# Linear attention's decay levels in three visits of TensorE a layer instead of four, and a rule for who waits for several PSUM banks

## The chip, the cores and the metric

The kernel runs on one core of a Trainium2 chip. The metric is device time in microseconds of one execution, the median of the runs. Five engines work side by side, each through a queue of its own: TensorE (PE in the profile, with its weight loads PEld), VectorE (DVE), ScalarE (ACT), GpSimd (POOL) and SyncE (SP), which here issues nearly all DMAs.

## The reference

Two layers over 256 positions of width 2048, all in float32. Each layer projects its input once and splits the result into three groups: chunked softmax attention (A, 8 heads), gated linear attention (B, 4 heads with keys of 64 and values of 128) and attention to 256 memory tokens (M, 4 heads). The outputs are gated, concatenated, projected, added to the residual and normalized. What matters here is the part of B inside a chunk of 64 positions:

```python
b = jnp.cumsum(gc, axis=1)
decay = jnp.exp(-jnp.abs(b[:, :, None] - b[:, None, :]))
attn = jnp.einsum('bihd,bjhd,bijhd->bhij', qc, kc, decay)
o_intra = jnp.einsum('bhij,bjhv->bihv', attn, vc)
```

The decay depends on i, j and the feature d, so the scores are not one product of matrices. The kernel splits the 64 x 64 pairs by levels. At a level of size s, the pairs (i, j) lie on the two sides of the middle of a block of 2s positions; with respect to that middle the decay is a product of a factor of i and a factor of j, so the level's scores are one product of decayed keys and decayed queries. Sizes 32, 16, 8, 4, 2 and 1 cover all pairs but the diagonal, which has no decay. That makes seven kinds: -1 (the diagonal) and levels 0 to 5. Each kind's product is computed for all pairs, and a mask picks those that belong to it.

## The kernel before, in words

**The stream of weights.** Nearly all time goes to products with weights. Each weight piece is loaded by DMA (`raw`), rounded by ACT to a high part `wh` (line 261) and completed by DVE with a low part `wl` (line 268). TensorE then multiplies the parts with the input's parts. `take()` hands out the next piece and keeps the high parts three and the low parts two pieces ahead. These operations carry a high priority, so that on ACT and DVE they go ahead of other work that is ready.

**Order.** The order of instructions on TensorE and on SP is the program's own. On ACT and DVE it is fixed when the program is built, by priority and by a forecast of when the operands are ready; on the chip each engine works through its queue in that order.

**Ticks.** After each weight piece the loop calls `tick()`. The smaller work is written as generators: each `next()` issues some instructions, and the number that it yields says after how many ticks it wants to go on. `tick()` first steps those `aside` (the generator `gla` of linear attention, and some helpers), then those `active`: at most two heads at a time, taken in order from `waiting`. `finish(gens)` ticks until the named generators are done; the first use of it in a layer's later part is in the gate of group B.

**Counting.** Call the moment of `beside(gens[0] + others)` tick 0. Ticks 1 to 8 belong to `values(2)`, 9 to 16 to `values(3)` (pieces of 388 columns), 17 to 24 to the projection of further heads, 25 to 32 to the memory queries, 33 on to the gates. Attention head pairs step at these ticks: scores (A) 9, 17, 25, 33; softmax one tick later; transposes of the weights (line 737) four ticks after A; values six ticks after A.

**`gla`.** Lines 533 to 709. It transposes the low-rank gate input, multiplies by the gate matrix, forms the running sums `b_` and, with `distance(lev)` (a subtraction on DVE, line 576, then abs and exp on ACT, lines 578 and 579) and `decayed(dd)` (two products on DVE, lines 584 and 585), the decayed keys and queries of a level. Then it visits TensorE four times, `VISITS`: kinds (-1, 0), (1, 2), (3, 4) and (5). In the first visit four transposes of the keys (line 606) go ahead, and ACT copies them out (line 607). A visit takes two banks `pb` (three in the last), issues 32 matmuls of 64 x 64 x 64 per kind into them, kind i in the columns from 256 i, and has DVE read the result: kind -1 by line 636, the others by a predicated copy, line 638, two of them per kind. The last visit also issues the state's products. After a visit the next visit's levels are prepared, a tick for each step. A tick after the last visit, the combining step takes four banks; a last step five ticks later transposes the result.

**Banks.** PSUM has eight banks; the smaller work shares banks 4 to 7, through the list `free`: `banks(n)` takes the first n, `release` appends them at the end. A bank that is taken again must have been read by whoever was to read it; the build adds the waits. The list is a matter of the program's order, not of time: it is run through while the program is written out. `scratch` gives one of eight rotating SBUF tiles.

In this kernel every caller of `banks` issues its matmuls and the reads of them and releases the banks within the same step, for instance

```python
pb, = yield from banks(1)
mm(ps[:, pb, 0:128], q[:, 0:128], k[:, 0:128], True, True)
mm(ps[:, pb, 128:384], q[:, 128:256], k, True, True)
s = scratch([P, 384])
dve.scalar_tensor_tensor(s, ps[:, pb, :384], SCALE, bias[h], op0=ALU.mult, op1=ALU.add)
release(pb)
```

Of the kernel before, what the change touches and what calls it, by code (L numbers as in the profile page):

```python
# [16 lines left out]
P = 128  # L17
# [3 lines left out]
CH = 64  # L21
# [3 lines left out]
RMS_EPS = 1e-6  # L25
SCALE = P ** -0.5
LEVELS = (32, 16, 8, 4, 2, 1)
VISITS = ((-1, 0), (1, 2), (3, 4), (5,))
PART_B = "WB" * 12
PART_A = "TW" * 16  # L30
QUARTERS = (3, 2)
# [21 lines left out]
def hybrid_trunk_kernel(  # L53
# [23 lines left out]
    ps = psp.tile([P, 8, 512], F32, name="ps")  # L77
# [3 lines left out]
    def nm(s):  # L81
        uid[0] += 1
        return f"{s}_{uid[0]}"

    def mm(o, l, r, start, stop):
        pe.matmul(o, l, r, start=start, stop=stop, skip_group_check=True)  # L86

    def scratch(shape, dtype=F32):
        return sc.tile(shape, dtype, name=nm("sc"), tag="sc")
# [33 lines left out]

    free = [4, 5, 6, 7]

    def banks(n):
        while len(free) < n:
            yield 1
        return [free.pop(0) for _ in range(n)]

    def release(*bs):
        free.extend(bs)
# [397 lines left out]
        later(pool.dma_start(ng, norm_g[l]))  # L530
        return gb, ng

    def gla(gb, ng, gq, gk, asv, yraw):
# [38 lines left out]
        def distance(lev):  # L572
            s = LEVELS[lev]
            bm = b_.rearrange("p (g c) -> p g c", c=2 * s)
            dd = scratch([P, 512])
            dve.tensor_tensor(dd.rearrange("p (g c) -> p g c", c=2 * s), bm,
                              bm[:, :, s - 1:s].to_broadcast([P, 512 // (2 * s), 2 * s]), op=ALU.subtract)
# [4 lines left out]
        def decayed(dd):  # L582
            kl = scratch([P, 512])
            dve.tensor_tensor(kl, gkf, dd, op=ALU.mult)
            dve.tensor_tensor(dd, gqf, dd, op=ALU.mult)
            return kl, dd

        dd = distance(0)
# [4 lines left out]
        dve.tensor_tensor(qe, gqf, eb, op=ALU.mult)  # L593
        yield 1
        ready = [(gkf, gqf), decayed(dd)]
        yield 3

        kdT = yraw[:, 0:2].rearrange("p h (g c) -> p (h g) c", c=P)
        st = hd.tile([P, 3, 2, P], F32, name=nm("st"), tag="st")
        for v, levels in enumerate(VISITS):  # L600
            last = v == len(VISITS) - 1
            if v == 0:
                pt, = yield from banks(1)
                for t in range(2):
                    for b in range(2):
                        pe.transpose(ps[:, pt, (t * 2 + b) * P:(t * 2 + b + 1) * P], kd[:, b * T + t * P:b * T + t * P + P], ident)  # L606
                act.copy(kdT, ps[:, pt].rearrange("p (g c) -> p g c", c=P))
# [12 lines left out]
            if last:  # L620
                kv = (pb[2], pb[1])
                for c in (0, 1, 2):
                    rs = slice((c % 2) * 64, (c % 2) * 64 + 64)
                    t = c // 2
                    for b in range(2):
                        for par in range(2):
                            h = 2 * b + par
                            mm(ps[par * 64:par * 64 + 64, kv[c % 2], (t * 2 + b) * P:(t * 2 + b + 1) * P],
                               kdT[rs, t * 2 + b, par * 64:par * 64 + 64],
                               asv[rs, t, 16 + h * P:16 + (h + 1) * P], True, True)  # L630
            for i, lev in enumerate(levels):
                o = 256 if last else i * 256
                for par in range(2):
                    pv = ps[:, pb[par], o:o + 256].rearrange("p (g c) -> p g c", c=CH)
                    if lev < 0:
                        dve.tensor_tensor(pairs[par], pv, eye.unsqueeze(1).to_broadcast([P, 4, CH]), op=ALU.mult)
                    else:
                        dve.copy_predicated(pairs[par], lmask[:, lev].unsqueeze(1).to_broadcast([P, 4, CH]), pv)
            if last:
                for c in range(3):  # L640
                    src = ps[:, kv[c % 2]].rearrange("p (g c) -> p g c", c=P)[:, (c // 2) * 2:(c // 2) * 2 + 2]
                    if c == 0:
                        dve.tensor_copy(st[:, 0], src)
                    else:
                        for b in range(2):
                            dve.scalar_tensor_tensor(st[:, c, b], st[:, c - 1, b], elast[:, b * 4 + c:b * 4 + c + 1],
                                                     src[:, b], op0=ALU.mult, op1=ALU.add)
            release(*pb)
            if not last:
                ready = []  # L650
# [15 lines left out]
        for g in range(4):  # L666
            t, b = g // 2, g % 2
# [5 lines left out]
        for odd, even in ((1, 2), (3, None)):  # L673
            for b in range(2):
                for c in (odd, even):
                    if c is not None:
                        for par in range(2):
                            rs = slice(par * 64, par * 64 + 64)
                            g = (c // 2) * 2 + b
                            mm(ps[place(par, c % 2), by[par], g * P:(g + 1) * P],  # L680
                               qe[rs, b * T + c * CH:b * T + (c + 1) * CH], st[rs, c - 1, b], True, True)
        for half in range(2):
            for par in range(2):
# [3 lines left out]
                o = on[par][hs, g0:]  # L687
# [12 lines left out]
        for par in range(2):  # L700
# [5 lines left out]
            o = ps[:, pt].rearrange("p (b t h c) -> p h b t c", b=2, t=2, h=2)  # L706
# [266 lines left out]
    gens = []  # L973
    for l in range(L):
        last = l == L - 1
# [32 lines left out]
        gq = hd.tile([P, 2, T], F32, name=nm("gq"), tag="gq")  # L1008
        gk = hd.tile([P, 2, T], F32, name=nm("gk"), tag="gk")
# [4 lines left out]
        gp = gla_inputs(l)  # L1014
        asv = per.tile([P, 2, 1552], F32, name=nm("asv"), tag="asv")
# [40 lines left out]
        yraw = [per.tile([P, 4, T], F32, name=nm("yr"), tag=f"yr{i}") for i in range(4)]  # L1056
# [212 lines left out]
```

## Time and profile before

| what | value |
|---|---|
| median of 3 runs | 912.76 us (912.55 to 913.89) |
| profiled execution, own time | 913.39 us |
| its span | 911.4 us |
| instructions | 14553 |
| mean granted TensorE clock | 0.999 |
| matmuls of linear attention's levels, 64 x 64 | 448 in two layers |

The span runs from the first to the last instruction of the profiled execution. "Busy" is the time in which an engine had an instruction under way; on TensorE successive matmuls overlap, so that the distance between two starts is a better measure of a cost than a duration. A row of the timeline gives the start, the duration from the first start to the last end of the merged instructions, engine, line, operation, output and operands, shape and count; in brackets stands the idle time ahead of it and what ended it. In the code a float32 matmul is one call; on TensorE it shows as two instructions. A row of the waits reads "who waits <- for whom: total us, times, longest".

### The profile page before, as it was taken

The page shows a single profiled execution, that of the slowest core. Times are in us where ns is not written, and L with a number is a line of the kernel's source. Part 1 is how long each engine was busy: PE and PEld are TensorE (multiplying, and loading weights), DVE is VectorE, ACT ScalarE, POOL GpSimd, SP SyncE. Part 2 cuts the span into 40 slices and gives each one's busy share as a digit, 9 for nine tenths or more (in the row PEclk, how much of TensorE's full clock was granted, in tenths as well). Part 3 has the DMA queues.
Part 4 walks back from the last instruction along what each step waited for, and adds up shares of the span by engine and source line. Part 5 has one row for each costly group of instructions (what it writes and reads, how often), then busy time and mean ns, then how long its engine had stood idle before and what let it go on. Part 6 is the DMA issues. An engine that isn't in the chain of part 4 may idle for free.

```text
span 911.4 us, 14553 instructions
## 1 busy us (share of the span) xinstructions
PE 903.2 (99%) x5491; PEld 795.3 (87%) x5491; DVE 717.9 (79%) x995; ACT 551.8 (61%) x809; POOL 13.6 (1%) x32
## 2 busy tenths in 40 slices
PE   9999999999999999999999999999999999999997
PEld 7889989998888888888888899999988888888885
DVE  5697688698766777799979767886886778778996
ACT  5675655576576675555559655556756667566540
POOL 1000000000000000000000000000000000100000
PEclk9999999999999999999999999999999999999999
DMA  8868786775445446876775787666754565776652
GB/s 298 293 195 288 262 266 206 236 253 180 160 145 161 159 161 187 289 272 223 236 243 167 206 291 254 223 196 186 218 177 134 178 192 185 273 277 232 229 190 93
DMA packets 64294, 196.21 MB, mean 215 GB/s; under 512 B 7008, under 2 KB 9568, under 8 KB 64224
## 3 DMA queue, kind: packets, MB, share of 16 engines
q1 hardware_dynamic: 63200, 193.08, 64.9%
q0 software_dynamic: 1024, 2.21, 0.8%
q8 instruction: 43, 0.70, 0.3%
q14 instruction: 27, 0.22, 0.1%
HBM read 193.16 MB, written 2.10 MB: 214 GB/s over the span
## 4 chain that ended last, share of the span: by engine, by line
PE 98%; DVE 1%; DMA 0%; ACT 0%; issue 0%; SPq 0%; DVEq 0%
PE ps L86 96%; PE ps L737 1%; DVE wl L268 0%; DMA raw<-w 0%; PE ps L833 0%; PE ps L775 0%; PE ps L704 0%; DVE sz L498 0%; DVE x L268 0%; ACT wh L261 0%; PE ps L606 0%; ACT res L877 0%; PE ps L541 0%; DVE term L260 0%; ACT wh L360 0%
## 5 line engine op out<-in xcount | busy, mean ns | idle before, releaser
L268 DVE TENSOR_TENSOR wl<-raw,wh 128x1024 fp32r<-128x1024 f32 (+1 forms) x313 | 364.8, 1169 | 118.5 <-PE ps L86 71.1
L261 ACT CAST wh<-raw 128x1024 fp32r<-128x1024 f32 (+1 forms) x313 | 313.9, 1008 | 233.4 <-PE ps L86 125.3
L86 PE MATMUL ps<-x,wh 128*128 128x512 f32 x1408 | 445.0, 397 | 0.0
L86 PEld LDWEIGHTS ps<-x,wl 128*128 128x128 f32 x1408 | 264.2, 188 | 63.2 <-DVE wl L268 1.0
L86 PE MATMUL ps<-x,wl 128*128 128x256 f32 x1408 | 277.5, 279 | 0.3 <-DVE wl L268 0.3
L86 PE MATMUL ps<-wh,x 128*128 128x512 f32 (+2 forms) x856 | 246.5, 369 | 0.9 <-ACT wh L360 0.9
L86 PEld LDWEIGHTS ps<-x,wh 128*128 128x128 f32 x1408 | 219.2, 189 | 1.6 <-issue 0.3
L86 PEld LDWEIGHTS ps<-wh,x 128*128 128x128 f32 x856 | 155.5, 188 | 19.7 <-ACT wh L360 1.1
L86 PE MATMUL ps<-wl,x 128*128 128x512 f32 (+2 forms) x428 | 157.8, 369 | 0.1
L86 PEld LDWEIGHTS ps<-wl,x 128*128 128x128 f32 x428 | 80.3, 188 | 10.5 <-DVE wl L268 0.6
L261 ACT CAST wh<-term 128x776 fp32r<-128x776 f32 (+1 forms) x39 | 36.0, 924 | 51.2 <-DVE term L260 43.3
L268 DVE TENSOR_TENSOR wl<-term,wh 128x776 fp32r<-128x776 f32 (+1 forms) x39 | 41.5, 1065 | 12.7 <-PE ps L86 12.0
L260 DVE TENSOR_TENSOR term<-term,term 128x776 f32<-128x776 f32 (+1 forms) x39 | 41.3, 1060 | 0.2 <-DMA term<-w 0.2
L86 PE MATMUL ps<-wh,s 128*128 128x512 f32 (+1 forms) x144 | 41.2, 367 | 0.0
L86 PEld LDWEIGHTS ps<-wh,s 128*128 128x128 f32 x144 | 25.8, 188 | 3.1
L86 PE MATMUL ps<-wl,s 128*128 128x512 f32 (+1 forms) x72 | 26.6, 370 | 0.3 <-DVE wl L268 0.3
L498 DVE SCALAR_TENSOR_TENSOR sz<-ps,sz 128x512 f32<-128x512 f32 x24 | 16.4, 687 | 5.0 <-ACT sz L497 4.1
L728 ACT ACTIVATE sc<-sc,mx 128x128 f32<-128x128 f32 (+1 forms) x32 | 14.2, 444 | 8.2 <-DVE mx L726 8.2
L86 PE MATMUL ps<-wh,sc 128*128 128x388 f32 x64 | 16.5, 338 | 0.0
L86 PEld LDWEIGHTS ps<-wl,s 128*128 128x128 f32 x72 | 13.5, 188 | 2.3 <-DVE wl L268 0.8
L1119 DVE TENSOR_TENSOR yr<-sz,yr 128x512 f32<-128x512 f32 x16 | 11.0, 687 | 4.6 <-ACT sz L1117 4.6
L1117 ACT ACTIVATE sz<-sz 128x512 f32<-128x512 f32 x16 | 10.1, 632 | 7.1 <-DVE sz L498 7.0
(222 smaller groups left out, 713.9 us busy)
## 6 DMA issues: line engine op xcount, KB each, us to landing
raw<-w SPq DMA_DIRECT2D x254, 512.0 KB, 4.3
raw<-w SPq DMA_DIRECT2D x64, 388.0 KB, 3.8
term<-w SPq DMA_DIRECT2D x24, 388.0 KB, 4.3
term<-w SPq DMA_DIRECT2D x15, 512.0 KB, 5.3
bias<-relw SPq DMA_DIRECT2D x16, 192.0 KB, 3.9
res<-xT SPq DMA_DIRECT2D x4, 512.0 KB, 6.9
res<-xn SPq DMA_DIRECT2D x4, 512.0 KB, 5.4
raw<-memT SPq DMA_DIRECT2D x4, 512.0 KB, 4.5
```

The source lines that it names most:

```text
L86: pe.matmul(o, l, r, start=start, stop=stop, skip_group_check=True)
L260: in_order(dve.tensor_tensor(d.raw, d.raw, d.plus, op=ALU.add))
L261: act.copy(d.hi, d.raw)
L268: in_order(dve.tensor_tensor(d.lo, d.raw, d.hi.bitcast(F32), op=ALU.subtract))
L498: dve.scalar_tensor_tensor(dst, a, scale, dst, op0=ALU.mult, op1=ALU.add)
L728: act.activation(s[:, own[t]], s[:, own[t]], AF.Exp, bias=mx[:, t:t + 1], accum_out=zs[:, t:t + 1])
L737: pe.transpose(ps[:, pt, i * P:(i + 1) * P], s[:, i * P:(i + 1) * P], ident)
L1117: act.activation(sz, sz, AF.Silu)
L1119: dve.tensor_tensor(yraw[i][:, j:j + 2], sz, yraw[i][:, j:j + 2], op=ALU.mult)
```

## The change

`VISITS` has three entries: (-1, 0, 1), (2, 3, 4) and (5). Visits 0 and 1 take four banks; the third kind goes to the second two of them. Level 1 is now prepared ahead of visit 0, two ticks before it, and one tick is added to the wait. Two of the tiles for the third level of visit 1 are halves of `yraw[3]` (the memory heads' output, written later) instead of scratch tiles. `banks` notes who asks for more than one bank in `wanted`, and whoever asks for one bank waits as long as somebody is noted there.

```diff
-VISITS = ((-1, 0), (1, 2), (3, 4), (5,))
+VISITS = ((-1, 0, 1), (2, 3, 4), (5,))
...
+    wanted = []
+
     def banks(n):
-        while len(free) < n:
+
+        if n > 1:
+            wanted.append(n)
+        while len(free) < n or wanted and n == 1:
             yield 1
+        if n > 1:
+            wanted.remove(n)
         return [free.pop(0) for _ in range(n)]
...
         ready = [(gkf, gqf), decayed(dd)]
-        yield 3
+        yield 2
+        ready.append(decayed(distance(1)))
+        yield 2
...
-            pb = yield from banks(3 if last else 2)
+            pb = yield from banks(3 if last else 4)
             for i, (lev, (kl, ql)) in enumerate(zip(levels, ready)):
-                o = 256 if last else i * 256
+                o = 256 if last else i % 2 * 256
...
-                                mm(ps[half * CH:(half + 1) * CH, pb[par], o + (t * 2 + b) * CH:o + (t * 2 + b + 1) * CH],
+                                mm(ps[half * CH:(half + 1) * CH, pb[i // 2 * 2 + par], o + (t * 2 + b) * CH:o + (t * 2 + b + 1) * CH],
                                    kl[rs, c0:c0 + CH], ql[rs, c0:c0 + CH], True, True)
...
-                    pv = ps[:, pb[par], o:o + 256].rearrange("p (g c) -> p g c", c=CH)
+                    pv = ps[:, pb[i // 2 * 2 + par], o:o + 256].rearrange("p (g c) -> p g c", c=CH)
...
-                for lev in VISITS[v + 1]:
-                    dd = distance(lev)
+                for n, lev in enumerate(VISITS[v + 1]):
+                    mine, other = (extra[:, h * 2:h * 2 + 2].rearrange("p h t -> p (h t)") if n == 2 else None for h in range(2))
+                    dd = distance(lev, mine)
                     yield 1
-                    ready.append(decayed(dd))
+                    ready.append(decayed(dd, other))
                     yield 1
                 yield 1
...
-        gens = [[gla(*gp, gq, gk, asv, yraw[0])]]
+        gens = [[gla(*gp, gq, gk, asv, yraw[0], yraw[3])]]
```

`distance` and `decayed` take an optional tile in which to put their result.

More of the change, by code (lines that the diff above doesn't have):

```diff
@@ L531, in gla_inputs, with gla @@
         return gb, ng
-    def gla(gb, ng, gq, gk, asv, yraw):
+    def gla(gb, ng, gq, gk, asv, yraw, extra):
         gqf = gq.rearrange("p b t -> p (b t)")
@@ L570, in gla, with distance @@
         act.activation(eb, b_, AF.Exp, scale=1.0 / 16)
-        def distance(lev):
+        def distance(lev, dd=None):
             s = LEVELS[lev]
             bm = b_.rearrange("p (g c) -> p g c", c=2 * s)
-            dd = scratch([P, 512])
+            if dd is None:
+                dd = scratch([P, 512])
             dve.tensor_tensor(dd.rearrange("p (g c) -> p g c", c=2 * s), bm,
@@ L580, in distance, with decayed @@
             return dd
-        def decayed(dd):
-            kl = scratch([P, 512])
+        def decayed(dd, kl=None):
+            if kl is None:
+                kl = scratch([P, 512])
             dve.tensor_tensor(kl, gkf, dd, op=ALU.mult)
@@ L631, in gla @@
             for i, lev in enumerate(levels):
-                o = 256 if last else i * 256
+                o = 256 if last else i % 2 * 256
                 for par in range(2):
-                    pv = ps[:, pb[par], o:o + 256].rearrange("p (g c) -> p g c", c=CH)
+                    pv = ps[:, pb[i // 2 * 2 + par], o:o + 256].rearrange("p (g c) -> p g c", c=CH)
                     if lev < 0:
```

## The prediction

> **What bounds the kernel now.** I read the page's busy table first, then the chain that ended last, then the waits of TensorE, then the timelines of the stretch that the edit touches.
>
> ```profile
> span 911.4 us, 14553 instructions
> PE 903.2 (99%) x5491; PEld 795.3 (87%) x5491; DVE 717.9 (79%) x995; ACT 551.8 (61%) x809; POOL 13.6 (1%) x32
> PE 98%; DVE 1%; DMA 0%; ACT 0%; issue 0%; SPq 0%; DVEq 0%
> ...
> PE ps L86 <- DVE eps L972: 1.2, 1, 1.2
> PE ps L86 <- ACT wh L360: 0.9, 1, 0.9
> PE ps L86 <- DVE wl L268: 0.6, 2, 0.3
> PE ps L86 <- ACT row L873: 0.3, 1, 0.3
> ```
>
> TensorE is the bound, and its waits come to 3.0 us in all. None has anything to do with linear attention. So a gain can come only from less time on TensorE, and any new wait of TensorE adds to the time one for one.
>
> I count the stages by ticks from `beside(gens[0] + others)`, one tick after each weight piece. In each tick the linear attention generator `gla` steps first, then the heads. The PE timeline confirms the count: visit 0 (tick 12), its heads' transposes (tick 13), visit 1 together with two new heads (17), visit 2 (22).
>
> ```profile
> 196.75 0.34 PE L86 MATMUL ps<-wl,x 128*128 128x388 f32 x1
> 196.93 0.60 PE L606 MATMUL ps<-ident,sc 128*128 128x128 f32 x4
> 197.46 0.69 PE L86 MATMUL ps<-gq,gk 64*64 64x64 f32 x32
> 197.98 0.65 PE L86 MATMUL ps<-sc,sc 64*64 64x64 f32 x32
> 198.55 0.62 PE L86 MATMUL ps<-wh,x 128*128 128x388 f32 x2
> ...
> 200.78 0.82 PE L737 MATMUL ps<-ident,sc 128*128 128x128 f32 x6
> ...
> 211.67 0.39 PE L86 MATMUL ps<-x,wl 128*128 128x256 f32 x2
> 211.99 1.16 PE L86 MATMUL ps<-sc,sc 64*64 64x64 f32 x64
> 213.08 1.58 PE L86 MATMUL ps<-qk,qk 128*128 128x128 f32 x8
> ...
> 228.40 0.63 PE L86 MATMUL ps<-x,wh 128*128 128x512 f32 x2
> 228.87 0.39 PE L86 MATMUL ps<-x,wl 128*128 128x256 f32 x2
> 229.19 1.16 PE L86 MATMUL ps<-sc,sc 64*64 64x64 f32 x64
> 230.28 0.73 PE L86 MATMUL ps<-x,wh 128*128 128x512 f32 x2
> 230.84 0.40 PE L86 MATMUL ps<-x,wl 128*128 128x256 f32 x2
> 231.08 0.64 PE L86 MATMUL ps<-x,wh 128*128 128x512 f32 x2
> ...
> 645.61 0.60 PE L606 MATMUL ps<-ident,sc 128*128 128x128 f32 x4
> ```
>
> What is to be seen: durations overlap, so a cost is the distance between starts. Thirty-two small matmuls (one kind) take 197.98 - 197.46 = 0.52 us, four transposes 0.53, and one weight piece of this stage 200.78 - 198.55 = 2.23, of which some 0.1 is the return from small matmuls; 2.1 without it.
>
> **The rule in `banks` does nothing.** No caller yields between taking banks and releasing them: `a_head`, `m_head`, `gla` and `norm_between` all release in the same step. So `free` holds all four banks whenever a step of a head or of `gla` begins, the `while` never loops for n > 1, and `wanted` is empty again before anybody else asks. Who goes first doesn't change. No instruction comes or goes: 7 kinds of 32 matmuls a layer before and after, the same DVE and ACT operations, no DMA added. What changes is the place of the steps and which banks they use.
>
> **The term that is saved.** Visits before: ticks 12, 17, 22, 25. After: 13, 20, 23 (one kind more is prepared at tick 11, then seven ticks between visits 0 and 1, three between 1 and 2). The rest of `gla` moves from 26 and 31 to 24 and 29. Heads keep their ticks (9, 13, 15, 17, 21, 23, 25, 29, 31). So small matmuls interrupt the weight stream in ten ticks between 12 and 31 instead of eleven. One visit alone costs: entry, 229.19 - 228.87 = 0.32 behind a pair that undisturbed takes 231.08 - 230.84 = 0.24, so 0.08; return, 230.84 - 230.28 = 0.56 for a pair that undisturbed takes 228.87 - 228.40 = 0.47, so 0.09. Together 0.17 a layer, **0.35 us** for two. (These two pairs are a quarter of a piece of the later stage: 4 x 0.71 = 2.8 us.)
>
> **The term that is added.** Banks are handed out first in, first out. Before, visit 0 takes two, and the heads of the next step take the other two. After, visit 0 takes all four (pb[0..3]) in tick 13, and in the same tick, right behind it on TensorE, heads 0 and 1 transpose their scores (L737) into pb[0] and pb[1]. These banks hold kinds -1 and 0 until DVE has read them: two L636, then two L638. TensorE must wait for the third of these four before the first head, and behind this wait stands the whole weight stream. So I need the time at which DVE gets there.
>
> ```profile
> 183.00:199.43 16.43, 16.43 (x32) 1.00 0.79 256
> 633.50:649.51 16.01, 16.01 (x31) 1.00 0.69 211
> ...
> 197.95 0.96 DVE L268 TENSOR_TENSOR wl<-raw,wh 128x776 fp32r<-128x776 f32 x1
> 198.83 0.68 DVE L585 TENSOR_TENSOR sc<-gq,sc 128x512 f32<-128x512 f32 x1
> 199.43 0.75 DVE L636 TENSOR_TENSOR pairs<-ps,eye 128x256 f32<-128x256 f32 x2
> 200.09 0.77 DVE L638 COPY_PREDICATED pairs<-lmask,ps 128x256 f32<-128x256 uint8 x2
> 201.04 0.97 DVE L268 TENSOR_TENSOR wl<-raw,wh 128x776 fp32r<-128x776 f32 x1 [0.18 <-issue]
> 201.93 0.69 DVE L576 TENSOR_TENSOR sc<-qb 128x512 f32<-128x512 f32 x1
> ...
> 649.51 0.75 DVE L636 TENSOR_TENSOR pairs<-ps,eye 128x256 f32<-128x256 f32 x2
> ```
>
> The windows show DVE without a gap for 16 us ahead of these reads, in both layers, so it reaches them by its backlog: at 199.43 and 649.51. Level 1's products (L584, L585) stand in that backlog already, so the edit doesn't lengthen it. But one more low-part subtraction (L268) comes due as the visit now stands one piece later, and it has priority: 201.93 - 201.04 = 0.89. DVE is then ready at 200.32 in layer 0 and 650.40 in layer 1. Three reads take 0.66 + 0.44 = 1.10: 201.42 and 651.50.
>
> TensorE, unstalled, begins visit 0 one piece later than before, at 196.93 + 2.1 = 199.03 and 645.61 + 2.1 = 647.71; transposes 0.53 and three kinds 1.61 bring it to the heads at 201.17 and 649.85. The waits are 0.25 and 1.65; with 0.05 to 0.1 for each release **0.35 and 1.7 us**. Layer 1 is the dearer because its DVE reaches the reads 649.51 - 199.43 = 450.08 us after layer 0's, and its TensorE visit 0 only 645.61 - 196.93 = 448.68: 1.4 us further behind.
>
> The Trainium skill's page "PSUM — Partial Sum Buffer" (section "PSUM bank collisions raise a hardware error") wants two engines kept apart on a bank and quadrant, reads against matmul writes too. By that the first read also waits until kind 0, which shares kind -1's bank, is written. In rows this is 199.03 + 0.53 + 1.09 = 200.65 instead of 200.32 in layer 0, so 0.7 us there, nothing in layer 1, and 0.3 on the sum. The trace of before can't decide: its first read stands at 199.43, after both kinds in any case.
>
> **Costs that the trace doesn't show, and their bounds.** The third kind's odd half goes to pb[3], the bank from which ACT must still copy the transposed keys (L607).
>
> ```profile
> 197.70 0.84 ACT L261 CAST wh<-raw 128x776 fp32r<-128x776 f32 x1 [0.50 <-DMA raw<-w]
> 198.44 0.58 ACT L607 COPY yr<-ps 128x512 f32<-128x512 f32 x1
> ...
> 648.10 0.58 ACT L607 COPY yr<-ps 128x512 f32<-128x512 f32 x1
> 650.17 1.05 ACT L261 CAST wh<-raw 128x1024 fp32r<-128x1024 f32 x1 [1.49 <-DMA raw<-w]
> ...
> 231.82 1.43 DVE L638 COPY_PREDICATED pairs<-lmask,ps 128x256 f32<-128x256 uint8 x4
> ...
> 245.96 1.10 PE L86 MATMUL ps<-asv,pairs 64*64 64x128 f32 x32
> 247.53 2.27 ACT L685 COPY sc<-ps 64x512 f32<-64x512 f32 x4
> 247.86 0.74 PE L86 MATMUL ps<-x,wh 128*128 128x512 f32 x2
> ```
>
> The copy ends 2.09 and 3.07 us after the transposes begin; TensorE wants the bank after 0.53 + 1.04 = 1.6. Below: nothing, if one cast of 0.85 alone stands ahead. Above: 0.5 and 1.5, and in layer 1 some 2.5 if the cast that waits for its DMA until 650.17 is put ahead (650.17 + 1.05 + 0.58 = 651.8 against 649.3). These waits lie ahead of the heads' wait on the same engine, so the longer of the two counts, not the sum; I take nothing on top.
>
> Three later neighbours are closer than before. Heads at tick 21 use visit 1's first banks a piece (2.8 us) after it: before, four reads ended 231.82 + 1.43 - 229.19 = 4.1 us after a visit's start, and the heads now come after 1.6 + 2.8 = 4.4. Heads at tick 25 use two banks of the combining step of tick 24: its copies ended 247.53 + 2.27 - 245.96 = 3.8 us after it began, wanted after 247.86 - 245.96 = 1.9, and a piece: 4.7. Level 1 must be ready for visit 0: L585 ends at 199.5 and about 649.6, the third kind stands at 200.6 and 649.3; at most 0.3, under the same longer wait. I take nothing for all three, and up to 0.5 each for the upper end. No SP or POOL work is moved; two scratch tiles become `yraw[3]`, free until the memory heads write it at tick 41 and later.
>
> **Sum.** -0.35 + 0.35 + 1.7 = +1.7 us. The profiled execution took 913.39 us (span 911.4 and 2.0 around it), 0.6 above the median of 912.76; its 915.1 is **914.4** by the median. A measurement of this kernel can tell about 0.2% (1.8 us) from no change, so the forecast stands just inside.
>
> **Rivals.**
> - *The wait is dearer.* A further subtraction (L576, 0.6 us for visit 1's levels) gets ahead of the reads, and in layer 1 the key copy waits for the late DMA: 0.95 + 2.5 - 0.35 = +3.1, and neighbours may add up to 1: 915.9 to 916.9. It decides when DVE reaches the first read later than 201.0 and 650.8. For it: DVE's order is fixed when the program is built, and it ran full there. Against: the L576 comes after the reads in the program.
> - *Nothing waits.* If DVE's reads come as early as the matmuls allow (200.08 + 1.1 = 201.2, no wait in layer 0) and layer 1 loses its lag, only the saving is left: 912.4; with layer 1's lag but no subtraction ahead, 649.51 + 1.10 - 649.85 = 0.8, so 913.2. For it: TensorE never waited for these reads before. Against: they stood 2 to 3 us behind their matmuls.
> - *The rule works as it says.* If heads were in truth held back, they would run a tick later; nothing waits for them before tick 36, so it would cost or save no more than one interruption: 912.2 to 912.8. The code speaks against it.
> - *Faster by over 0.2%* would need 1.8 us out of a saving of 0.4; only a changed order elsewhere could give it.
>
> **Chances.** Forecast (net +0.9 to +2.6): 0.50. Dearer: 0.22. Nothing waits, or the rule works (-0.6 to +0.9): 0.24. Faster by more: 0.04. The forecast's upper third and the dearer rival make slower by over 0.2% 0.44; faster by over 0.2% 0.04; within 0.2% 0.52. The range takes in the saving alone and the dearer rival: **912.2 to 916.9**.
>
> **What would show it.** In the waits of TensorE, a new row of L737 for DVE L638, once a layer, the longer in layer 1; or one of L86 for ACT L607. In the PE timeline, 96 small matmuls (32 of gq,gk and 64) ahead of L737 at about 199.6, 64 and 32 alone later, one interruption fewer. Wrong would be: no wait there and the time within 0.4 us of before; a wait over 2 us in layer 0; or TensorE waiting for weights.

## The result, and the profile after

| what | before | after |
|---|---|---|
| median of 5 runs each | 912.76 us (912.37 to 914.18) | 921.96 us (920.25 to 923.33) |
| ratio | | 1.0096, 95% interval 1.0084 to 1.0107 |
| profiled execution, own time and span | 913.39, 911.4 us | 923.16, 921.4 us |
| mean granted TensorE clock | 0.999 | 0.995 |

The change costs 9.2 us by the medians and 8.8 by the ratio (7.7 to 9.8 by its interval). The forecast was 914.4 with a range up to 916.9: the time lies outside it, on the side of slower, and the loss is more than five times the +1.7 of the sum. In the first experiment below two of six executions took 1505.6 and 4792.5 us, and its ratio is made without them.

**Where the time went.** Two lines mark the stages: the transposes at the head of linear attention (L541 before, L548 after) and those of the memory heads' scores (L775 and L787), which come behind the whole of linear attention. These are the answers on one line's instructions, for the kernel before and then the kernel after. A row gives the count, the durations, and the starts of the first (in layer 0) and the last (in layer 1).

```profile
L541 PE MATMUL ps<-ident,asv x4: 272/272/273, 171.8 to 620.6; 128*16 128x128 f32 x4
L775 PE MATMUL ps<-ident,sc x32: 272/273/273, 305.8 to 778.4; 128*128 128x128 f32 x32
```

```profile
L548 PE MATMUL ps<-ident,asv x4: 272/272/273, 173.6 to 625.4; 128*16 128x128 f32 x4
L787 PE MATMUL ps<-ident,sc x32: 272/273/273, 311.2 to 788.4; 128*128 128x128 f32 x32
```

Layer 0 between its marks: 305.8 - 171.8 = 134.0 before, 311.2 - 173.6 = 137.6 after, so +3.6. Layer 1: 157.8 and 163.0, so +5.2. The stretch between is 0.6 shorter, the end (911.4 - 778.4 and 921.4 - 788.4) takes 133.0 in both. The start is 1.8 later; in the profiles of the experiments below, which share this start, the mark moves between 171.1 and 173.4, so nearly all of that part is what the start varies by. The loss sits twice in the stretch of linear attention. These two stretches, 134.0 and 157.8 us before, serve as a measure in the experiments too: they leave the start out.

**The waits of TensorE** after the change; before, none had to do with linear attention.

```profile
PE ps L86 <- DVE sc L594: 1.8, 2, 1.1
PE ps L749 <- DVE pairs L649: 1.7, 2, 1.3
...
PE ps L86 <- DVE wl L275: 1.0, 2, 0.7
PE ps L86 <- ACT yr L618: 0.9, 1, 0.9
...
```

Three names are new. L749, the heads' transposes, waits for the reads of visit 0's banks, as forecast. L594 is the product that makes level 1's decayed queries, the third kind's operand. L618 is ScalarE's copy of the transposed keys, out of the bank that the third kind's odd half needs. The timeline of TensorE at visit 0, after, in both layers, puts them in order:

```profile
200.88 0.60 PE L617 MATMUL ps<-ident,sc 128*128 128x128 f32 x4
201.41 0.69 PE L86 MATMUL ps<-gq,gk 64*64 64x64 f32 x32
201.93 0.65 PE L86 MATMUL ps<-sc,sc 64*64 64x64 f32 x32
203.27 0.33 PE L86 MATMUL ps<-sc,sc 64*64 64x64 f32 x2 [0.69 <-DVE sc L594]
204.46 0.69 PE L86 MATMUL ps<-sc,sc 64*64 64x64 f32 x30 [0.86 <-ACT yr L618]
205.62 1.54 PE L749 MATMUL ps<-ident,sc 128*128 128x128 f32 x6 [0.47 <-DVE pairs L649]
206.81 1.00 PE L86 MATMUL ps<-wh,x 128*128 128x388 f32 x2
...
656.30 1.09 PE L86 MATMUL ps<-sc,sc 64*64 64x64 f32 x32 [1.10 <-DVE sc L594]
658.65 1.13 PE L749 MATMUL ps<-ident,sc 128*128 128x128 f32 x6 [1.25 <-DVE pairs L649]
```

The first two kinds run. Then the third waits for its operand, two of its matmuls go into the free bank, the other thirty wait for the key copy, and the heads wait for the reads. In layer 0 that is 0.69 + 0.86 + 0.47 = 2.0 us. In layer 1 it is 1.10 + 1.25 + a wait of 0.74 for a low part at 651.65, in the weight piece ahead of the visit, = 3.1. So 2.0 of 3.6 and 3.1 of 5.2 are waits. The rest shows in the last two rows of layer 0: the transposes take 1.54 and the pair of weight products behind them 1.00, where such a pair undisturbed takes 0.52. The windows of the profile after (length, busy time of PE, PEld, DVE, ACT and POOL, granted clock, DMA share, GB/s) say why:

```profile
202.00:204.00 2.00, 0.90 (x42) 0.62 (x34) 2.00 (x7) 1.13 (x2) 0.00 (x0) 1.00 0.85 274
204.00:206.00 2.00, 1.07 (x32) 0.94 (x33) 2.00 (x8) 0.93 (x2) 0.00 (x0) 0.79 0.91 283
206.00:208.00 2.00, 2.00 (x10) 2.00 (x9) 2.00 (x5) 1.12 (x3) 0.00 (x0) 0.50 0.56 227
208.00:210.00 2.00, 2.00 (x12) 2.00 (x10) 1.15 (x3) 1.26 (x3) 0.00 (x0) 0.85 0.00 0
...
658.00:660.00 2.00, 1.35 (x8) 1.32 (x9) 2.00 (x6) 0.66 (x2) 0.00 (x0) 0.79 0.82 272
660.00:662.00 2.00, 2.00 (x8) 2.00 (x7) 1.38 (x3) 1.40 (x3) 0.00 (x0) 0.50 0.28 111
662.00:664.00 2.00, 2.00 (x12) 2.00 (x11) 1.43 (x2) 1.08 (x2) 0.00 (x0) 0.86 0.00 0
```

In layer 0 TensorE is busy 0.90 and 1.07 of two times 2.00 us, and then the granted clock falls to half: 2 x (0.21 + 0.50 + 0.15) = 1.7 us of full-speed work are lost, which is some 3.4 us at half speed. The loss is a little less as TensorE idles for a part of the first of these slices. Layer 1 gives the same 1.7. In the kernel before the clock is 1.00 in all these windows. Waits and clock together are 3.7 against the 3.6 of layer 0, and 4.8 against the 5.2 of layer 1.

**Why the operand and the reads are late.** VectorE has no gap ahead of these reads, before and after, so its order decides. From its timeline after the change, layer 0:

```profile
185.42 1.22 DVE L572 TENSOR_TENSOR_SCAN qb<-sc,sc 128x512 f32<-128x512 f32 x1
...
188.61 0.69 DVE L584 TENSOR_TENSOR yr<-qb 128x512 f32<-128x512 f32 x1
...
194.79 0.70 DVE L593 TENSOR_TENSOR yr<-gk,yr 128x512 f32<-128x512 f32 x1
...
196.98 0.69 DVE L594 TENSOR_TENSOR yr<-gq,yr 128x512 f32<-128x512 f32 x1
...
200.52 0.70 DVE L584 TENSOR_TENSOR sc<-qb 128x512 f32<-128x512 f32 x1
...
202.00 0.55 DVE L744 TENSOR_SCALAR sc<-sc,zs 128x128 f32<-128x128 f32 x2
...
202.53 0.68 DVE L594 TENSOR_TENSOR sc<-gq,sc 128x512 f32<-128x512 f32 x1
203.12 0.97 DVE L275 TENSOR_TENSOR wl<-raw,wh 128x776 fp32r<-128x776 f32 x1
204.00 0.55 DVE L744 TENSOR_SCALAR sc<-sc,zs 128x128 f32<-128x128 f32 x2
204.45 0.76 DVE L647 TENSOR_TENSOR pairs<-ps,eye 128x256 f32<-128x256 f32 x2
205.12 1.44 DVE L649 COPY_PREDICATED pairs<-lmask,ps 128x256 f32<-128x256 uint8 x4
```

The three operations whose output is `yr` are level 4's. Level 4 belongs to visit 1 and is written in the program after visit 0, yet its subtraction stands at 188.61, ahead of everything of level 1. Its tiles lie in `yraw[3]`. A tile from `scratch` is one of eight in rotation and has to wait until its last reader is done; `yraw[3]` has no reader at that point that is still to come, and its input, the running sums, has been there since 185.42 + 1.22 = 186.64. Levels 2 and 3 have the same input but scratch tiles, and their subtractions stand at 200.52 and 207.04. The build orders VectorE by priority and by when operands are ready. So the likely reading is that it put level 4's operations where the free tile made them ready: 3 x 0.6 us of VectorE (and two operations of ScalarE) ahead of level 1's decayed keys and queries, of the heads' scaling and of the reads.

The first read (L647) stands at 204.45. Counted from the mark L541 or L548, to leave the start out, that is 204.45 - 173.6 = 30.9, against 199.43 - 171.8 = 27.6 before and 200.32 - 171.8 = 28.5 by the forecast. It is 2.3 us later than forecast: 1.8 for level 4, and 0.6 for the subtraction of level 2 at 200.52, which also stands ahead of the reads and stood behind them before.

Two theories at this point: **A**, level 4 pulled ahead is the loss, and with it in place the forecast's sum comes true; **B**, level 4's place doesn't matter, and visit 0 with four banks is the whole loss by itself, through the key copy's bank and the heads behind it. A third part, **C**, is the halved clock, which makes any cluster of waits dearer than its idle time.

### The profile page after: what moved, and what is told of

Same layout as the page of the kernel before. It is cut to its first block, busy times and chain, and to the rows that moved or that the text cites. A ratio compares the mean times of both kernels' runs of the same rounds, so it can differ in the third digit from the quotient of the medians.

```text
span 921.4 us, 14573 instructions
## 1 busy us (share of the span) xinstructions
PE 908.8 (99%) x5491; PEld 800.5 (87%) x5491; DVE 717.1 (78%) x995; ACT 552.5 (60%) x809; POOL 13.4 (1%) x32
## 4 chain that ended last, share of the span: by engine, by line
PE 94%; DVE 2%; DMA 1%; ACT 1%; issue 1%; SPq 0%; DVEq 0%; ACTq 0%
PE ps L86 93%; DMA raw<-w 1%; DVE wl L275 1%; PE ps L749 1%; PE ps L845 0%; PE ps L787 0%; ACT wh L268 0%; PE ps L716 0%; DVE mx L738 0%; DVE sc L744 0%; DVE pairs L647 0%; ACT L563 0%; DVE qb L572 0%; DVE sz L505 0%; DVE yr L594 0%
## 5 line engine op out<-in xcount | busy, mean ns | idle before, releaser
L86 PE MATMUL ps<-wh,x 128*128 128x512 f32 (+2 forms) x856 | 250.2, 374 | 0.6 <-ACT wh L367 0.6
L86 PEld LDWEIGHTS ps<-wh,x 128*128 128x128 f32 x856 | 158.6, 192 | 19.5 <-ACT wh L367 0.8
L86 PE MATMUL ps<-w,x 128*128 128x512 f32 (+1 forms) x72 | 14.3, 356 | 0.0
```

## The experiments

Each ratio is to runs of the kernel before on the same chip. Their medians are 912.91 us for experiments 2, 3, 4 and the first run of 1; 913.56 for the second run of 1 and for 5, 6 and 7; and 912.63 for 8, 9 and 10. Across these groups the ratios are the safer comparison. Where a text says by how much the stretches grew, it is the two stretches of the profiled execution against those of the kernel before.

**1. Level 4 held in its place.** The subtraction into `yraw[3]` is put behind what the program issued before it on VectorE; nothing else changes.

```diff
+            held = behind if mine_ else lambda i: i
-            dve.tensor_tensor(dd..., op=ALU.subtract)
+            held(dve.tensor_tensor(dd..., op=ALU.subtract))
```

> The changed kernel with one edit: the first DVE operation of level 4 (its subtraction into the tile in yraw[3]) may not be issued ahead of the DVE work that stands before it in the program. Theory A (backlog): the tile in yraw[3] depends on nothing, so level 4 was issued 15 us early and its three products of 0.6 us each pushed level 1 and the reads of visit 0 back by 1.8 us. Then TensorE's wait for level 1 (0.69 and 1.10 us) and for the low part in layer 1 (0.74) go, the reads come at about 202.6 and 655.7, the heads wait 0.8 and 1.9 us, and the time is 914.5 to 917, the upper end if the clock is still halved in layer 1. Theory B (banks alone): level 4's place doesn't matter, 921 to 923. The forecast on record (0.35 and 1.7 us of waits) gives 914.4.

Measured: ratio 1.0057 (1.0040 to 1.0073), from four executions of 917.87 to 920.40 us. The profile is of the one that took 4792.5 us, where a weight product takes 1624 ns instead of 397 at a recorded clock of 1.000; why is not known. As it says nothing about the waits here, the kernel was run again:

> [...] In this kernel DVE's queue has the heads' softmax in the place that it had in the kernel before. Theory A: the heads' own products come in time again, level 1 too, and what is left is the bank wait of the prediction, 0.5 to 0.9 us in layer 0 and 1.7 to 2.2 in layer 1, together with the late key copy, plus up to 1.5 us in a layer for the halved clock if these waits bring it; 917 to 920.

Measured: 917.77 us, ratio 1.0050 (1.0032 to 1.0068). By the two ratios 3.6 to 4.2 us of the 8.8 go, so A is a part, and not all. VectorE's order is now that of the kernel before (the softmax's scaling at 196.13, before at 196.42), but for level 2's subtraction, which at 197.66 still stands ahead of the reads. TensorE's waits have another name. Its waits, and ScalarE's timeline in layer 0:

```profile
PE ps L86 <- ACT yr L620: 4.6, 2, 2.8
...
PE ps L86 <- DVE sc L596: 0.8, 1, 0.8
```

```profile
200.89 1.05 ACT L268 CAST wh<-raw 128x1024 fp32r<-128x1024 f32 x1 [1.71 <-DMA raw<-w]
201.84 0.62 ACT L589 ACTIVATE sc<-sc 128x512 f32<-128x512 f32 x1
202.37 0.57 ACT L620 COPY yr<-ps 128x512 f32<-128x512 f32 x1
```

The key copy (L620) is 0.57 us of work, but it stands behind a weight cast that waits 1.71 us for its DMA, and behind an exponential. It ends at 202.94 and the third kind goes on at 202.99, after 2.75 us; in layer 1 after 1.85. The heads then wait for nothing: by that time their banks are read. This profile can't price the hold, though. It is of an execution of 920.84 us, 3.1 over this kernel's median; its stretches grew by 4.0 and 4.4, nearly as much as the changed kernel's 3.6 and 5.2, and the clock falls in it as well (0.50 at 204 to 206 and 0.51 at 658 to 660). Experiments 5 and 8 price it better.

**2. Visit 0 a tick later, level 4 still early.** The heads' transposes of tick 13 now go ahead of visit 0.

```diff
         ready.append(decayed(distance(1)))
-        yield 2
+        yield 3
...
-                yield 1
+                if v:
+                    yield 1
```

> The changed kernel with visit 0 one tick later (tick 14) and one tick less behind it, so that visit 1 stays at tick 20; level 4 is still issued early. The heads' transposes of tick 13 now stand ahead of visit 0, and a whole weight piece (2.1 us) stands between visit 0 and the next user of its banks. Theory A and theory B both: the waits shrink by about a piece each, level 1's to nothing; 912.4 to 914.5. If the time stays above 918, neither adjacency nor lateness at tick 13 is the cause, but something else that the three visits bring.

Measured: 920.87 us, ratio 1.0081 (1.0066 to 1.0096); both theories had it at 914.5 at most. The wait for the reads is gone, and in its place stands

```profile
PE ps L750 <- DVE sc L745: 4.4, 4, 1.3
```

The heads' transposes wait for the heads' own softmax (L745): VectorE scales it at 200.71 and 202.71 instead of 196.42. VectorE, held up by level 4's early work, is late for whatever TensorE wants next, so moving one consumer only changes who waits. The stretches grew by 2.7 and 5.5.

**3 and 4. The kernel before, its first visit at tick 13.** Two kinds as before, no `yraw[3]`, no third kind: first with four banks taken for visit 0, then with two.

```diff
         ready = [(gkf, gqf), decayed(dd)]
-        yield 3
+        yield 4
...
-            pb = yield from banks(3 if last else 2)
+            pb = yield from banks(3 if last else 2 if v else 4)
...
-                yield 1
+                if v:
+                    yield 1
```

> The kernel before with visit 0 (still kinds -1 and 0) at tick 13, right ahead of the heads' transposes, and with four banks taken, so that the heads get the two banks which DVE must still read. No level 1 in the visit, no tile in yraw[3]. This is the bank term of the prediction by itself: reads from 200.1 and about 649.2, third read 1.1 later, heads due at 200.65 and 649.35: waits of 0.5 and 1.0 us, 913.5 to 915.5. If theory B holds (banks explain all 9 us), 919 or more.

Measured: 916.10 us, ratio 1.0027 (1.0017 to 1.0036). The new wait, then rows of TensorE's timeline, then rows of VectorE's, in layer 0:

```profile
PE ps L738 <- DVE pairs L638: 2.4, 2, 1.2
...
201.74 0.65 PE L86 MATMUL ps<-sc,sc 64*64 64x64 f32 x32
203.59 0.89 PE L738 MATMUL ps<-ident,sc 128*128 128x128 f32 x6 [1.21 <-DVE pairs L638]
...
202.44 0.76 DVE L636 TENSOR_TENSOR pairs<-ps,eye 128x256 f32<-128x256 f32 x2 [0.52 <-PE ps L86]
```

Here it is VectorE that waits for TensorE. Kind -1, whose row starts at 201.22, is written at 201.22 + 0.69 = 201.91, and kind 0 at 201.74 + 0.65 = 202.39. VectorE stands idle for 0.52 us and begins with kind -1 at 202.44, when both are there; in layer 1 it is idle for 0.20. So the heads' wait of 1.21 in this kernel is the length of three reads, 1.10, with two releases, and no backlog.

> The same as the run with four banks, but visit 0 takes two, as in the kernel before: the heads right behind it take the other two banks and needn't wait for its reads. All theories: 912.3 to 913.3, no wait of TensorE at the heads' transposes; the difference to the run with four banks is the price of the bank collision.

Measured: 916.32 us, ratio 1.0032 (1.0019 to 1.0045). Of this kernel, the wait in TensorE's timeline and ScalarE's timeline:

```profile
204.53 0.55 PE L738 MATMUL ps<-ident,sc 128*128 128x128 f32 x3 [1.73 <-ACT yr L607]
```

```profile
202.95 1.04 ACT L261 CAST wh<-raw 128x1024 fp32r<-128x1024 f32 x1 [2.69 <-DMA raw<-w]
203.90 0.58 ACT L607 COPY yr<-ps 128x512 f32<-128x512 f32 x1
```

Both ran slower than expected (913.5 to 915.5, and 912.3 to 913.3). With four banks the wait at the forecast's place appears alone, 1.2 us in each layer; the time, +2.5 by the ratio and +3.2 by the medians, is nearly the forecast's two terms of 0.35 and 1.7. With two banks the reads cost nothing, but the bank of the key copy comes round to the second head, and it waits 2.6 us in two layers for the same copy, behind the same kind of cast. So **B** as the whole loss is out (it had 919 or more), but a part of it holds without any third kind: in both kernels, at tick 13, heads right behind visit 0 find one bank that somebody slow is to empty.

**5. Level 4 held and visit 0 a tick later**, both edits above.

> Level 4 held back and visit 0 at tick 14, behind the heads. Theory A: with both causes gone (the heads' products aren't pushed back by level 4, and nobody takes visit 0's banks right behind it) no wait over 0.7 us is left in layer 0, the clock stays, and the time is within 2 us of the kernel before: 912.4 to 915. Theory B (banks alone): the same as the run at tick 14 with level 4 early, 920 to 921.

Measured: 915.61 us, ratio 1.0020 (1.0011 to 1.0029), 0.6 over the expected range. The waits for softmax and reads are gone; what is left is the key copy, in front of the third kind, 1.02 and 1.43 us, where theory A had none over 0.7 in layer 0:

```profile
PE ps L86 <- ACT yr L620: 2.5, 2, 1.4
```

The clock is 1.00 in all windows of this stretch. This kernel differs from that of experiment 2 by the hold alone. The ratio falls from 1.0081 to 1.0020, some 5.6 us, and the stretches grew by 2.3 us in all instead of 8.1. So here the traces show the price of level 4's early place: longer waits, and in layer 1 of experiment 2 a clock of 0.50 as well.

**6 and 7. The clock by itself.** Products of the identity with itself, into an accumulator bank that is idle then, are put where TensorE waits: six ahead of the third kind and three ahead of the heads. Nothing reads them.

```diff
+            def fill(n):
+                for _ in range(n):
+                    mm(ps[:, 2 - side[0], :P], ident, ident, True, True)
...
+                if v == 0 and i == 2:
+                    fill(6)
...
+            if v == 0:
+                fill(3)
```

> The changed kernel with nine matmuls of the identity (128 x 128, results unused) ahead of the places where TensorE waits in visit 0: six ahead of the third kind (about 1.2 us), three ahead of the heads (0.6). They do no work that is wanted. Theory C (the waits also cost a halved clock for some 3 us in each layer): the fill stands in time that was waited anyway and keeps TensorE busy, the granted clock stays at 1.00, and the time falls by 1.5 to 3.5 us against the changed kernel, to 918.5 to 920.5. Without theory C it stays at 921 to 924.

Measured: 919.68 us, ratio 1.0063 (1.0050 to 1.0075). TensorE does more and is done sooner. The windows of this kernel, at the places that had 0.50 above:

```profile
206.00:208.00 2.00, 2.00 (x13) 2.00 (x12) 1.38 (x3) 1.57 (x2) 0.00 (x0) 1.00 0.08 23
...
660.00:662.00 2.00, 2.00 (x13) 1.97 (x12) 1.79 (x3) 1.46 (x3) 0.00 (x0) 1.00 0.00 0
```

So C holds: 2.3 us by the medians (921.96 - 919.68) and 3.0 by the ratios (1.0096 and 1.0063) come back when the array is kept at work through the same waits; the stretches grew by 6.81 instead of 8.75 us, 1.9 less. It is less than the 3.4 of the windows, since the fill costs some time of its own: in layer 0 it and the wait that is left take 1.53 + 0.77 + 0.23 = 2.5 us, where the waits alone took 2.0. With level 4 held as well (four and six of them):

> Level 4 held back, and four such matmuls ahead of the third kind and six ahead of the heads. Theory C: if the halved clock is in the run without the fill, it goes here and the time falls by 1 to 3 us against that run, to 916 to 918; if the clock is full there, the fill only adds its 2 us less the waits, 0 to 1.5 us slower.

Measured: 919.48 us, ratio 1.0056 (1.0042 to 1.0070), where the held kernel alone gave 917.77. A miss: ahead of the heads the held kernel has no wait to fill, and the six products there take 206.29 - 204.85 = 1.4 us in layer 0. The clock is 1.00 in all windows of this kernel's stretch. How much the clock gave back here isn't shown, since the profile of the held kernel is of an execution well over its median.

**8. The key transposes a tick ahead of visit 0**, so that their copy has a piece more of time.

```diff
         ready.append(decayed(distance(1)))
-        yield 2
+        yield 1
...
                 release(pt)
+                yield 1
             pb = yield from banks(3 if last else 4)
```

With level 4 held:

> Level 4 held to program order as in the run that holds it alone (917.77 us, waits of TensorE for ScalarE's key copy 4.6 us in 2), and the four key transposes one tick ahead of visit 0, so that the copy of their bank is done when the third kind wants it. Theory (the bank of the key copy is what visit 0 waits for, once level 4 is back in its place): the waits for the key copy go; what is late next are the two heads' transposes, which wait for VectorE's reads of visit 0's banks, 2.0 to 2.8 us in 2 as in the kernel with two kinds and four banks (2.4), and level 1's operand with up to 1 us in a layer; one interruption more a layer costs 0.2 each; granted clock 0.9 or better at visit 0: 914.8 to 916.8 us. Rival (the key copy is not the cause but only the last of several things late at that tick): the time stays at 917.3 to 918.5 with the waits under another name and the clock still near 0.5.

Measured: 916.70 us, ratio 1.0042 (1.0028 to 1.0055), in the theory's range. The key copy is done at 197.19 + 0.58, and TensorE's waits are

```profile
PE ps L752 <- DVE pairs L652: 2.0, 2, 1.2
...
PE ps L86 <- DVE sc L596: 0.8, 1, 0.8
```

The heads wait for the reads again, 0.84 and 1.20 us, and level 1's operand is late in layer 1. VectorE has no gap ahead of these reads, so this is the wait by backlog that was forecast. Without holding level 4:

> The changed kernel with nothing but the four key transposes one tick earlier. Theory: the wait for the key copy (0.86 us in layer 0, hidden in layer 1 behind the wait for level 1's operand) goes, but level 1's operand and the heads' reads stay as late, because level 4 is still ahead of them in VectorE's queue: the heads' wait grows by what the other gives back, one interruption more costs 0.2 a layer, the clock stays near 0.5 to 0.8: 920.5 to 922.5 us. Rival (the key copy's bank is the whole loss): 913 to 915 us.

Measured: 920.23 us, ratio 1.0085 (1.0072 to 1.0098), 0.3 under the theory's range; the rival, by which the key copy is the whole loss, is out. The key copy leaves the list, the other two grow (TensorE's waits):

```profile
PE ps L750 <- DVE pairs L650: 3.3, 2, 1.7
PE ps L86 <- DVE sc L594: 2.2, 2, 1.5
```

These two kernels are a second pair that differs by the hold alone: 1.0085 and 1.0042, some 3.9 us, and stretches that grew by 5.8 and 2.4. The granted clock is 1.00 in the stretches of both profiles, so in this pair the 3.5 us are waits and not the clock.

**9. All three mended**: level 4 held, visit 0 at tick 14, and the key transposes left at tick 13 together with the heads' transposes.

> Level 4 held, visit 0 at tick 14, and the key transposes left at tick 13, in one interruption with the heads' transposes. Theory (three things cost: level 4 pulled ahead, the heads' transposes right behind visit 0, the key copy's bank): all three are gone, TensorE waits for the key copy 0 to 0.3 us instead of 2.5, the clock is 1.00, and 2.5 us of the 915.61 go: 912.3 to 913.6 us, which is the time before or 0.4 us under it. Rival (three kinds in a visit cost by themselves, by a later VectorE queue or by later level 2 operands): waits move to the second visit or to the reads, 914.5 to 916 us.

Measured: 915.23 us, ratio 1.0022 (1.0012 to 1.0031). The theory's 912.3 to 913.6 is missed, and the rival holds: the range, and waits that move to the reads. Visit 0 now runs through without a wait (the 96 matmuls from 203.53 to 205.16), and the wait has gone one step further down, in TensorE's timeline:

```profile
208.49 1.57 PE L86 MATMUL ps<-sc,asv 128*128 128x256 f32 x8 [1.01 <-DVE pairs L652]
...
657.05 1.57 PE L86 MATMUL ps<-sc,asv 128*128 128x256 f32 x8 [0.81 <-DVE pairs L652]
```

These are the heads' value products of tick 15. They ask for banks, find those of visit 0, and wait for VectorE's reads of it. No version beat the kernel before. One more move, the value products a tick later, was not tried. The waits that it could save are 1.8 us; this kernel stands 2.6 above the one before by the medians, 2.0 by the ratio (1.1 to 2.8), and its stretches grew by 1.6. So whether that move would end ahead of the kernel before is open.

**10. Without the rule.** `banks` as before, the rest as changed.

```diff
-        if n > 1:
-            wanted.append(n)
-        while len(free) < n or wanted and n == 1:
+        while len(free) < n:
             yield 1
-        if n > 1:
-            wanted.remove(n)
```

> The changed kernel without the list wanted: whoever asks for one bank takes it if one is free, as before. Theory (no single-bank request falls between a four-bank request and its grant, so that the rule decides nothing): 920.3 to 923.3 us, as the changed kernel (921.96). Rival (the rule holds heads back and that is part of the loss): below 919.5 us.

Measured: 921.67 us, ratio 1.0089 (1.0073 to 1.0104), that of the changed kernel (1.0084 to 1.0107) within the noise.

## Why the prediction was wrong, step by step

**Right: what bounds the kernel.** TensorE's new waits add one for one. In experiment 3, at full clock, waits of 1.21 and 1.21 us stand in stretches that grew by 1.24 and 1.25. In the changed kernel waits of 2.0 and 3.1 stand in stretches that grew by 3.6 and 5.2, and nearly all of the rest is TensorE's own clock.

**Right: the rule in `banks` does nothing.** In experiment 10 its absence makes no difference, 921.67 against 921.96.

**Not seen: the saving of 0.35.** Counted as the prediction counts, experiment 3 has one interruption fewer in each layer, and its stretches grew by just its waits, within 0.04 us, with no sign of the 0.17. But the kernels of experiments 5 and 9, which have as many interruptions as the kernel before, come out 0.07 to 0.13 under their waits in each layer. So amounts of this size can't be told apart here, and the saving stays open.

**Right place, the sum near by luck: the heads' wait for the reads** ("0.35 and 1.7 us"). With three kinds, level 4 held and an early key copy (experiment 8) it is 0.84 and 1.20, behind a VectorE without a gap, as forecast; in layer 1 another 0.84 goes to level 1's operand just ahead. Layer 0 was priced too low and layer 1 too high, and the two errors nearly cancel. With two kinds (experiment 3) it is 1.21 in either layer, and there not by the backlog: VectorE waited for kind 0 to be written before it read kind -1. That is the order on which the prediction put 0.3 us more in layer 0 and left undecided. With the third kind's 0.52 between, its 0.7 and the 1.21 agree.

**Wrong: "Level 1's products (L584, L585) stand in that backlog already, so the edit doesn't lengthen it."** This is the step that failed first and cost most. It looked at the operations that the visit uses and not at those that the edit lets run earlier. The two tiles of `yraw[3]` were priced at nothing, as "free until the memory heads write it". The build took level 4, some 1.8 us of VectorE, ahead of level 1's products, the softmax and the reads, and level 2's subtraction, 0.6, ahead of the reads too; the first read came 2.3 us later than forecast. Level 1's operand, priced at "at most 0.3", made TensorE wait 0.69 and 1.10. Three pairs of kernels that differ by the hold alone show the price: 3.6 to 4.2 us (experiment 1), 5.6 (2 and 5) and 3.9 (8). In the last pair the clock is full in both profiles. That the free tile is the reason for the early place is argued from the build's rule and from levels 2 and 3; no run gave level 4 a scratch tile. Experiment 2 shows that moving the visit by a tick doesn't dodge it.

**Wrong: the key copy's bank, "These waits lie ahead of the heads' wait on the same engine, so the longer of the two counts, not the sum; I take nothing on top."** That the longer counts is right: in experiment 1 the key copy's wait leaves the heads none. But the longer one was the key copy, with 2.75 and 1.85 us where the bounds were 0.5 in layer 0 and 2.5 in layer 1. The upper end had the right mechanism, a cast that waits for its DMA put ahead of the copy, and gave it to layer 1 only. ScalarE's queue had been built anew, and rows of the old order were no bound. In the changed kernel itself both waits appear in turn in layer 0 (0.86 and 0.47); there the reads end last.

**Missing: the clock.** The forecast priced waits as idle time alone. Clustered, they halved the clock, at a price of some 3.4 us for both layers by the windows; experiment 6 recovered 1.9 to 3.0, by the way of counting. The Trainium skill, page "TensorE: Matmul & The Clock Gate", section "What's actually happening", puts the fall to half rate after at least one idle window of about 3.4 us; its section "HAM oscillation — how this bites in real kernels" makes of this a rule against idle gaps longer than that. By that rule the waits of the changed kernel, none over 1.3 us, would not have mattered. The trace agrees on the half (0.50), and its slow stretch of some 3.4 us is as long as the window that this page of the Trainium skill names. It differs on what sets it off: partly busy windows (0.90 and 1.07 of 2.00) were enough.

The rivals fared so: "the wait is dearer" had the right sign, and both things that it named came true: a late cast ahead of the key copy (0.99 us of waiting for its DMA in layer 0), and one subtraction more ahead of the reads, though it comes after them in the program. It stopped at 916.9, since it counted that subtraction and not a whole level, nor the clock. "Nothing waits" and "the rule works" are out. (The forecast's last step is 912.76 + 1.7 = 914.5 and not 914.4, which changes nothing.)

What stays open: how the remaining 4 to 5 us divide between the key copy, the reads and the clock. The experiments take them one at a time, and each time the next one in line grows, so the parts don't add up.

## What to carry to other kernels

Where the build orders an engine by readiness, a tile without an earlier reader may not be neutral: its work can move to the front of a full queue, so list what an edit lets run earlier, not only what it delays. A step that takes all banks of a rotation makes every later step wait for the slowest reader of any of them, and mending one wait shows the next; price the whole line of steps behind it. Where several short waits fall within a few microseconds of TensorE, add the price of a halved clock to the upper end; here it was up to 1.7 us each time.

## What the hardware showed that was not expected

Waits of 0.69, 0.86 and 0.47 us within 4 us halved TensorE's clock for some 3.4 us. Single waits of similar or greater length did not: 1.02 and 1.43 us in experiment 5 and 1.2 in experiment 3 passed with a clock of 1.00. A single one of 2.75, in the profile of experiment 1, did. It isn't a matter of idle time alone either. One profiled execution of the kernel with early key transposes passed at 1.00 (its own time 917.80, its median 920.23) with these windows:

```profile
200.00:202.00 2.00, 1.26 (x72) 0.98 (x63) 2.00 (x7) 1.13 (x2) 0.00 (x0) 1.00 0.85 285
202.00:204.00 2.00, 0.40 (x4) 0.37 (x5) 2.00 (x8) 0.45 (x1) 0.00 (x0) 1.00 0.88 274
204.00:206.00 2.00, 2.00 (x15) 2.00 (x14) 2.00 (x5) 1.04 (x3) 0.00 (x0) 1.00 0.65 236
```

TensorE was busy 1.66 of 4.00 us there, less than the 1.97 that lost the clock in the changed kernel. In layer 1 of the same execution waits of 1.54 and 1.65 us follow each other within 4 us, and the clock stays at 1.00 too. The same page of the Trainium skill calls the window free-running: it doesn't start anew with the kernel. A fall that depends on how the waits lie against such a window would fit this case. No run here moved the waits against the window on purpose, so this is a reading and not shown.
